# Sixty one-element vector writes ahead of the first transpose of a DMA-fed rotation kernel

## The chip, the cores and the metric

The kernel runs on one core of a Trainium2 chip. The metric is the device time of one execution in microseconds (us); lower is better. It reads about 1.8 us more than the span that the profile shows (124.01 us against 122.2 us for the profiled run of the kernel before). The vector engine is called DVE. The engines whose queues issue transfers are SP (here all loads but two) and ACT (here all stores, and two early loads).

## The reference

The program turns 96 images of 256 x 256 32-bit numbers by 90 degrees. It is pure data movement: 25.17 MB in and 25.17 MB out.

```python
def setup_inputs():
    batch, c, h, w = 32, 3, 256, 256
    return {"x": np.random.randn(batch, c, h, w).astype(np.float32)}

def reference(x):
    return np.rot90(x, k=1, axes=(-2, -1)).astype(np.float32)
```

## The kernel before

The 96 images are cut into six groups of 16 (4 MB each). A group is loaded into a tile `S`, transposed on the DVE in blocks into a tile `U`, and stored from `U`. The rest of the rotation lies in the address patterns. Three buffers exist for each of `S` and `U`. The first and the last group (kind 1) work in four 1 MB parts with one large transpose each. The four groups between (kind 2) use two 2 MB loads, 16 small transposes and two 2 MB stores. I call the transposes of kind 1 large and those of kind 2 small, and number the groups 0 to 5.

```python
    in_pool = ctx.enter_context(tc.tile_pool(name="in_pool", bufs=3))
    out_pool = ctx.enter_context(tc.tile_pool(name="out_pool", bufs=3))

    for g, kind in enumerate(KINDS):          # KINDS = [1, 2, 2, 2, 2, 1]
        S = in_pool.tile([P, F], fp32, name="S")
        U = out_pool.tile([P, F], fp32, name="U")
        if kind == 1:
            # ... (views cut)
            for s in range(4):
                eng = nc.scalar if g == 0 and s % 2 else nc.sync
                eng.dma_start(out=Sv[:, s], in_=xv[s])
            for s in range(4):
                # ... (src and dst: views of Sv[:, s] and Uv[:, s])
                nc.vector.transpose(dst, src)
                nc.scalar.dma_start(out=ov[s], in_=Uv[:, s])
        else:
            # ... (views cut)
            for b in range(2):
                nc.sync.dma_start(out=Sv[:, b], in_=xv[b])
            for q in range(R):                # R = 16
                nc.vector.transpose(dst[:, q], src[:, q])
            for a in range(2):
                nc.scalar.dma_start(out=ov[a], in_=Uv[:, a])
```

The framework schedules these instructions: it orders each engine's list by its own estimate of when things are ready, and it adds the semaphore waits.

## Time and profile before

| | before |
|---|---|
| time, median of the first 3 runs | 124.03 us (123.91 to 124.1) |
| span in the profile | 122.2 us |
| DVE busy | 91.5 us (75%) |
| bytes moved | 50.34 MB, mean 412 GB/s |

These are lines of the page of the kernel before. The DMA row gives, for each of 40 equal slices of the span, how busy the 16 DMA engines were in tenths (9 means 90% or more); the DVE row does so for the DVE.

```profile
span 122.2 us, 172 instructions
DVE 91.5 (75%) x72; POOL 0.2 (0%) x4
DVE  0039999729999999996599993199999999548000
DMA  4999999999999999999999999999999999999993
DMA packets 4610, 50.34 MB, mean 412 GB/s; under 512 B 513, under 2 KB 513, under 8 KB 513
```

The DMA row has no hole between its first and its last slice; the DVE row has five. The DVE's timeline puts times to them. Its columns are start, length from the first start to the last end, engine, line, operation, output and input, how many, and in brackets how long the engine sat idle before and what ended that.

```profile
8.17 15.44 DVE L50 STREAM_TRANSPOSE U<-S 128x2048 f32<-128x2048 f32 x4 [8.17 <-DMA S<-in_x_dram]
26.77 30.22 DVE L66 STREAM_TRANSPOSE U<-S 128x512 f32<-128x512 f32 x32 [3.16 <-DMA S<-in_x_dram]
59.34 15.20 DVE L66 STREAM_TRANSPOSE U<-S 128x512 f32<-128x512 f32 x16 [2.35 <-DMA S<-in_x_dram]
78.88 15.20 DVE L66 STREAM_TRANSPOSE U<-S 128x512 f32<-128x512 f32 x16 [4.33 <-issue]
93.93 11.61 DVE L50 STREAM_TRANSPOSE U<-S 128x2048 f32<-128x2048 f32 x3
108.69 3.97 DVE L50 STREAM_TRANSPOSE U<-S 128x2048 f32<-128x2048 f32 x1 [3.15 <-DMA S<-in_x_dram]
```

The DVE waits 8.17 us for the first load and then 3.16, 2.35, 4.33 and 3.15 us. The DMA engines hardly wait at all. The table of stretches shows it for the longest run of transposes; its columns are the stretch, its length, busy time of DVE and POOL (with the number of instructions), granted clock, DMA share and GB/s.

```profile
26.80:57.00 30.20, 30.19 (x32) 0.00 (x0) 1.00 1.01 432
```

### The profile page before, as it was taken

Reading aid. Unit: us, or ns where it says so; the run is one execution under the profiler, and the core shown is the slowest. Engines: PE = TensorE matmul, PEld = TensorE weight load, DVE = VectorE, ACT = ScalarE, POOL = GpSimd, SP = SyncE. Lnnn points to the kernel's source line nnn. Section 1 sums busy time; section 2 is a strip of 40 time slices with the busy share of each in tenths; the row PEclk is TensorE's granted clock in tenths of the full one; section 3 lists DMA queues with packets and bytes.
Section 4 is the critical chain, followed back from the end, with each engine's and each line's share of the span. In section 5 each row is a group of like instructions: output and inputs, shape, how many; then the busy total and the mean of one; then the engine's idle time right before and its main releaser. Section 6 shows DMA issues by size and latency. Waiting matters only on the chain.

```text
span 122.2 us, 172 instructions
## 1 busy us (share of the span) xinstructions
DVE 91.5 (75%) x72; POOL 0.2 (0%) x4
## 2 busy tenths in 40 slices
DVE  0039999729999999996599993199999999548000
POOL 0000000000000000000000000000000000000000
DMA  4999999999999999999999999999999999999993
GB/s 83 418 426 429 445 343 432 464 424 402 426 469 397 429 434 434 429 429 434 429 440 429 429 434 434 424 418 445 418 432 445 402 453 410 464 426 397 426 429 142
DMA packets 4610, 50.34 MB, mean 412 GB/s; under 512 B 513, under 2 KB 513, under 8 KB 513
## 3 DMA queue, kind: packets, MB, share of 16 engines
q10 hardware_dynamic: 2592, 27.26, 52.5%
q1 hardware_dynamic: 2016, 23.07, 45.2%
q14 instruction: 2, 0.01, 0.0%
HBM read 25.17 MB, written 25.17 MB: 412 GB/s over the span
## 4 chain that ended last, share of the span: by engine, by line
DMA 62%; DVE 27%; SPq 1%; issue 1%; DVEq 0%
DMA S<-in_x_dram 46%; DVE U L66 24%; DMA out_dram<-U 16%; DVE U L50 3%; SPq L45 1%; SPq L61 1%; DVEq L66 0%
## 5 line engine op out<-in xcount | busy, mean ns | idle before, releaser
L66 DVE STREAM_TRANSPOSE U<-S 128x512 f32<-128x512 f32 x64 | 60.6, 1050 | 9.8 <-DMA S<-in_x_dram 5.5
L50 DVE STREAM_TRANSPOSE U<-S 128x2048 f32<-128x2048 f32 x8 | 31.0, 3950 | 11.3 <-DMA S<-in_x_dram 11.3
L83 POOL MEMSET const-uint8-127<- 128x1 uint8 x1 | 0.1, 102 | 0.0
L83 POOL MEMSET const-bfloat16-1.0<- 128x1 bf16 x1 | 0.1, 101 | 0.0
L83 POOL MEMSET const-float32-0.0<- 128x1 f32 x1 | 0.1, 98 | 0.2 <-issue 0.2
L83 POOL MEMSET const-float32-1.0<- 128x1 f32 x1 | 0.1, 98 | 0.0
## 6 DMA issues: line engine op xcount, KB each, us to landing
S<-in_x_dram SPq DMA_DIRECT2D x8, 2048.0 KB, 25.0
out_dram<-U ACTq DMA_DIRECT2D x8, 2048.0 KB, 18.0
out_dram<-U ACTq DMA_DIRECT2D x8, 1024.0 KB, 15.0
S<-in_x_dram SPq DMA_DIRECT2D x6, 1024.0 KB, 26.5
S<-in_x_dram ACTq DMA_DIRECT2D x2, 1024.0 KB, 9.9
```

Source lines behind the costliest of these rows:

```text
L45: eng.dma_start(out=Sv[:, s], in_=xv[s])
L50: nc.vector.transpose(dst, src)
L61: nc.sync.dma_start(out=Sv[:, b], in_=xv[b])
L66: nc.vector.transpose(dst[:, q], src[:, q])
L83: nc = _bacc.Bacc("TRN2", target_bir_lowering=False, num_devices=1)
```

## The change

The intent is to put 60 tiny writes, with no use of their own, on the DVE ahead of its first transpose, and to see what they cost.

```diff
     out_pool = ctx.enter_context(tc.tile_pool(name="out_pool", bufs=3))
+
+    spare = ctx.enter_context(tc.tile_pool(name="spare", bufs=1)).tile([1, 1], fp32, name="spare")
+    for i in range(60):
+        nc.vector.memset(spare, 0.0)
```

All 60 write the same element, so each but the first waits on a semaphore for the one before. They do not all end up ahead of the first transpose: the scheduler places 31 ahead of it, one after each of the first three large transposes, and 26 between the fourth and the first small one.

## The prediction

> **What bounds the kernel.** DMA. The page moves 50.34 MB at a mean of 412 GB/s; its DMA row by slices stands at 9 tenths from slice 2 to 39, and a table of stretches gives 431-432 GB/s while the DVE transposes (26.8-57.0, 59.3-74.5, 78.9-109.0 us). 50.34 MB at 432 GB/s is 116.5 us of the 122.2 us span; the rest is start and tail. The DVE is busy 91.5 us (75%) and idle five times (timeline): 8.17 us before its first transpose, 3.16 at 26.77, 2.35 at 59.34, 4.33 at 78.88, 3.15 at 108.69. The chain of waits is 62% DMA, 27% DVE; the DVE part from 26.77 to 57.0 is on it only because the next load waits for a free buffer, while loads already queued keep the DMA full. The Trainium skill, "DMA: Bandwidth & Descriptors", section "Issuing engines are not separate DMA queues", says that all issuers share the same 16 DMA engines; the trace agrees (DMA share at most 1.02). So only the byte count and gaps in DMA work set the time.
>
> **What the change does.** It adds 60 one-element DVE memsets; bytes, transposes and DMAs stay. In the built order 31 stand ahead of the first transpose, one between each pair of the first four, and 26 between the fourth and the first small transpose. Nearly every memset waits on the DVE's own semaphore, so they run in series.
>
> **Cost.** No DVE memset is in the trace. POOL memsets last 98-102 ns; a transpose's end reaches the DMA issue in about 0.05 us (start 8.17, 3.95 long, issue at 12.17). The Trainium skill, "Perfetto Trace Analysis", section "Optimizing Scalar/DVE Operations", gives about 60 ns for a DVE access to SBUF, twice that in the profile. Estimate from these: 0.17 us per memset in series (0.06 to 0.25), 10 us for 60.
> - 31 ahead: from about 0.7 to 6 us, inside the 8.17 us wait: free.
> - 3 between: the fourth transpose ends about 0.4 us later, and so do stores.
> - 26 after: from about 24.0 to 28.4 us; the load they'd have waited for lands at 26.67. The first small transpose begins 1.6 us later (0 to 4).
>
> **How much is on the critical path.** That 1.6 us reaches the end of the second small group (57.0 to 58.6 us), then goes into the 2.35 us wait at 59.34; what passes goes into the 4.33 us at 78.88. Meanwhile the DMA stays fed: when the first group's stores are issued (42.0), the last earlier store lands at 45.8 and loads in flight at 49.5 and 59.2; when the later load and stores are issued (57.0), others land at 59.2 to 78.7. Nothing reaches the end.
>
> **Prediction: 124.1 us**, range 123.5 to 125.0; faster 0.01, same 0.97, slower 0.02.
>
> **What the profile would show.** DVE busy up by 3-8 us; 60 memsets of about 0.1 us, 0.1-0.25 us start to start; first transpose still at 8.2 us, its wait still ended by the load; first small transpose at about 28.4 us with its wait gone; the wait near 59 us under 1 us; DMA row and bytes as before; last load landing within 0.5 us of 108.7.
>
> **What would make it wrong.** Memsets over 0.24 us in series: the first transpose is late too, and the later shift exceeds 3.6 us. A delayed store or load that lets the DMA go dry, or another interleaving of the two queues that lands the last load later: the tail after it (13.5 us) follows one for one.

## The result, and the profile after

The changed kernel took 124.02 us (median of 6 runs, 123.94 to 124.19), the kernel before 123.97 us (6 runs, 123.91 to 124.1). The ratio is 1.0003, with a 95% interval of 0.999 to 1.0016. A ratio is the mean time of one kernel's fast runs over that of the other's of the same rounds, so not quite the ratio of the medians. The two kernels take the same time.

These are the page's lines of the changed kernel that answer to those above. The last one is the group of the writes: count, busy time, mean length in ns, idle time before them.

```profile
span 122.2 us, 231 instructions
DVE 95.1 (78%) x132; POOL 0.2 (0%) x4
DVE  3239999859999999997399996099999999766000
DMA  4999999999999999999999999999999999999993
DMA packets 4609, 50.34 MB, mean 412 GB/s; under 512 B 512, under 2 KB 512, under 8 KB 512
L37 DVE MEMSET spare<- 1x1 f32 x60 | 3.5, 59 | 3.8 <-PEq L89 0.8
```

The DVE is 3.6 us busier, and the DMA row is the same digit for digit. The DVE's timeline of the changed kernel up to the second group of waits:

```profile
0.79 3.46 DVE L37 MEMSET spare<- 1x1 f32 x31 [0.79 <-PEq L89]
8.14 7.84 DVE L56 STREAM_TRANSPOSE U<-S 128x2048 f32<-128x2048 f32 x2 [3.89 <-DMA S<-in_x_dram]
...
19.79 6.78 DVE L37 MEMSET spare<- 1x1 f32 x27
26.92 30.40 DVE L72 STREAM_TRANSPOSE U<-S 128x512 f32<-128x512 f32 x32 [0.35 <-DMA S<-in_x_dram]
60.08 15.21 DVE L72 STREAM_TRANSPOSE U<-S 128x512 f32<-128x512 f32 x16 [2.76 <-DMA S<-in_x_dram]
```

The first 31 writes end at 4.25 us (0.79 + 3.46), inside the wait for the first load, which shrinks from 8.17 to 3.89 us of idle time. The next transpose starts at 8.14 us as before. The 27 of the other line (the one after the third transpose, and the 26) end at 26.57 us, and the first small transpose starts at 26.92 us against 26.77 us. One write in the chain takes (3.46 - 0.06) / 30 = 0.113 us from start to start, though it is only 0.059 us long.

So the writes as built delay the first small transpose by only about 0.2 us. (The third small group starts 0.7 us later, at 60.08 us; the second traces below come back to it.) That leaves two explanations of why it is free:

- **Theory (spare time, DMA bound).** The DMA engines set the time. The DVE may be late by microseconds as long as they do not run dry; its later waits take the delay up.
- **Rival (a close fit).** The writes are free only because they end 0.1 us before the DVE may go on anyway. Any more would come out one for one.

### The profile page after: what moved, and what is told of

Its sections match the earlier page's. It is cut to its first block, busy times and chain, and to the rows that moved or that the text cites. A ratio compares the mean times of both kernels' runs of the same rounds, so it can differ in the third digit from the quotient of the medians.

```text
span 122.2 us, 231 instructions
## 1 busy us (share of the span) xinstructions
DVE 95.1 (78%) x132; POOL 0.2 (0%) x4
## 4 chain that ended last, share of the span: by engine, by line
DMA 67%; DVE 15%; issue 10%; SPq 0%
DMA S<-in_x_dram 51%; DMA out_dram<-U 15%; DVE U L72 8%; DVE U L56 7%; SPq L51 0%; DVE spare L37 0%
## 5 line engine op out<-in xcount | busy, mean ns | idle before, releaser
L37 DVE MEMSET spare<- 1x1 f32 x60 | 3.5, 59 | 3.8 <-PEq L89 0.8
```

Source lines behind the costliest of these rows:

```text
L37: nc.vector.memset(spare, 0.0)
```

## The experiments

Nine kernels were built on the kernel before. All results were correct.

### 44 and 60 writes between the first two groups

```diff
+            if g == 1:
+                for i in range(60):            # e_mid60; 44 in e_mid44
+                    nc.vector.memset(dst[0:1, :, 0, 0, 0], 0.0)
             for q in range(R):
                 nc.vector.transpose(dst[:, q], src[:, q])
```

Each write touches one element in every piece that the 16 transposes write, so none of these can start before all writes are done.

> All 60 writes (16 elements each, in one chain) stand between the fourth large transpose and the first small one. Theory (spare time of the DVE in later waits): 60 x 0.113 = 6.8 us from about 23.6 to 30.4, the first small transpose begins near 30.4 instead of 26.8 (3.6 us late), the 2.4 us wait near 59 vanishes, the 4.3 us wait near 79 shrinks by about 1 us, the DMA row stays full, time 124.0 (+-0.3). Rival (one for one: the writes were free only because they ended 0.1 us before the load they share the gap with landed): 127.6 us.

Measured (run e_mid60): 123.89 us against 124.0 us, ratio 0.9992 (0.9977 to 1.0006). The first small transpose started at 31.68 us, 4.9 us late (a 16-element write took 0.140 us from start to start, not 0.113). The rival's one for one is wrong. But the scheduler, seeing the writes, had also assigned the completion semaphores of several transfers anew, so loads waited for other things than before. The second run takes that away: with 44 writes, order and waits of all transfers are those of the kernel before.

> As e_mid60 with 44 writes: the count up to which the order and the waits of every DMA stay those of the kernel before, so that only the delay differs. In e_mid60 one write took 139 ns start to start, so 44 end at 23.4 + 6.1 = 29.5 us and the first small transpose is 2.7 us late. Theory: the 2.2 us wait near 59 takes it up, the one near 79 the rest, DMA row full, time 124.0 (+-0.3). Rival (e_mid60 was free only because its DMA waits were arranged anew; with the old ones the delay comes out one for one): 126.7 us.

Measured (e_mid44): 124.1 us against 123.96 us, ratio 1.0009 (0.9992 to 1.0025). Here is the DVE's timeline of this run:

```profile
8.56 15.44 DVE L50 STREAM_TRANSPOSE U<-S 128x2048 f32<-128x2048 f32 x4 [8.56 <-DMA S<-in_x_dram]
23.93 6.11 DVE L67 MEMSET U<- 1x16 f32 x44
30.08 45.26 DVE L69 STREAM_TRANSPOSE U<-S 128x512 f32<-128x512 f32 x48
76.65 15.17 DVE L69 STREAM_TRANSPOSE U<-S 128x512 f32<-128x512 f32 x16 [1.31 <-issue]
91.70 11.58 DVE L50 STREAM_TRANSPOSE U<-S 128x2048 f32<-128x2048 f32 x3
105.73 3.97 DVE L50 STREAM_TRANSPOSE U<-S 128x2048 f32<-128x2048 f32 x1 [2.44 <-DMA S<-in_x_dram]
```

The first small transpose is 3.3 us late (30.08 against 26.77), and not 2.7 as expected; in this trace the first transpose itself starts 0.4 us later than in that of the kernel before (8.56 against 8.17), after the wait for its load. Then 48 small transposes run in one piece where the kernel before had 32, a wait, and 16: the wait near 59 us is gone. The wait near 79 us has shrunk from 4.33 to 1.31 us. The fourth small group and the last transpose even start *earlier* than before: 76.65 against 78.88 us, and 105.73 against 108.69 us (107.54 in a second trace of the kernel before). The DVE's delay holds back stores, and loads that are already queued land earlier; a likely reason is that they then get more of the shared DMA engines, but no run tells that apart from other effects. The page's DMA row of this run:

```profile
DMA  4999999999999999999999999999999999999993
```

It is the row of the kernel before. The theory holds, in the clean case. What this run does not show is a delay too long for the later waits of the DVE to take up: those of the kernel before add up to 9.8 us after the first small transpose.

### 60 and 120 writes forced ahead of the first transpose

```diff
+            if g == 0:
+                for i in range(120):           # 60 in e_ahead60
+                    nc.vector.memset(Uv[0:1, :, 0:1], 0.0)
             for s in range(4):
                 # src, dst
                 nc.vector.transpose(dst, src)
```

> All 60 writes really ahead of the first transpose (4 elements each, one chain): they end at 0.8 + 60 x 0.113 = 7.6 us, before the load lands at 8.1. Theory and rival agree on 124.0; the first transpose at 8.2, the first small one at 26.8, so no trace of the writes after 8 us.

Measured (e_ahead60): 123.89 us against 124.01 us, ratio 0.9986 (0.9971 to 1.0001). The writes ended at 7.93 us and the first transpose started at 8.48 us, after a wait that the load ended. That is later than the expected 8.2, but in the traces with no write ahead of it the first transpose starts anywhere from 7.79 us (e_wait120) to 8.56 us (e_mid44). So 60 writes fit into the first wait; this run does not part the theories.

> 120 writes (4 elements each, one chain), all ahead of the first transpose: first transpose at 0.8 + 120 x 0.113 = 14.4 us instead of 8.2, so all stores of the first group 6.2 us late. Theory: the 16 DMA engines have 12.6 MB of loads (29 us) queued without any store, so they don't run dry; the 6.2 us go into the waits at 26.8, 59 and 79 (3.2 + 2.4 + 4.3 us); time 124.0 to 124.5. Rival (one for one beyond the first wait): 130.2 us.

Measured (e_ahead120): 124.56 us against 124.0 us, ratio 1.0047 (1.0032 to 1.0062). The first transpose started at 15.17 us, 7.0 us late (a 4-element write took 0.120 us from start to start), and 0.56 us of that reached the end. The rival's 130.2 us is far off. The theory's upper end, 124.5 us, was just missed. The 64 small transposes now run without any wait (from the timeline of this run):

```profile
0.79 14.34 DVE L48 MEMSET U<- 1x4 f32 x120 [0.79 <-PEq L86]
15.17 15.44 DVE L53 STREAM_TRANSPOSE U<-S 128x2048 f32<-128x2048 f32 x4
30.50 60.29 DVE L69 STREAM_TRANSPOSE U<-S 128x512 f32<-128x512 f32 x64
```

In both of these runs the scheduler had also rearranged the waits of transfers, so where the 0.56 us came from stays open.

### 60 writes without the chain

```diff
+    spare = ctx.enter_context(tc.tile_pool(name="spare", bufs=1)).tile([1, 60], fp32, name="spare")
+    for i in range(60):
+        nc.vector.memset(spare[:, i:i + 1], 0.0)
```

> 60 one-element writes to 60 different elements, so none waits on the one before; all stand ahead of the first transpose. If the 113 ns start to start of the changed kernel came from the chain of semaphore waits: about 60 ns start to start or less, the last write near 4.5 us. If it is the engine's own cost: still 113 ns, the last near 7.5 us. Time 124.0 either way, the first transpose at 8.2 us with its wait ended by the load.

Measured (e_free60): 123.97 us against 124.01 us, ratio 1.001 (0.9978 to 1.0042). From the timeline of this run:

```profile
0.79 1.72 DVE L34 MEMSET spare<- 1x1 f32 x60 [0.79 <-PEq L86]
8.69 15.44 DVE L53 STREAM_TRANSPOSE U<-S 128x2048 f32<-128x2048 f32 x4 [6.17 <-DMA S<-in_x_dram]
```

All 60 end at 2.51 us: (1.72 - 0.06) / 59 = 0.028 us each from start to start, though a record is still 0.059 us long, so they overlap. The chain costs the difference, 0.113 - 0.028 = 0.085 us per write. The expectation was about 0.06 us from start to start, or less. The first transpose started at 8.69 us and not at 8.2, 6 us after the last write and still after a wait that the load ended.

### The same writes after the last load

If DVE time is free because the DMA engines are busy meanwhile, it must cost something where they are about to run out of work: after the last load. A one-element copy that reads the last load makes the writes wait for it. Order and waits of all transfers are those of the kernel before.

```diff
+                if g == 5 and s == 3:
+                    nc.vector.tensor_copy(Uv[0:1, 3, 0:1], Sv[0:1, 3, 0:1])
+                    for i in range(60):        # 30 in e_tail30, 120 in e_tail120
+                        nc.vector.memset(Uv[0:1, 3, 0:1], 0.0)
                 nc.vector.transpose(dst, src)
```

> The same 60 one-element writes, but after the last load has landed (a one-element copy reads it first) and before the last transpose. Theory: last transpose 6.9 us late (115.6 instead of 108.7), its store issued at 119.6 instead of 112.7, when the other stores have just landed, so alone: about 4.5 us to landing, end of the span near 124.8 instead of 122.2, time near 126.5 (+2.0%, range 125.8 to 128). Rival A (DVE writes are free anywhere because DMA bounds the kernel): 124.0. Rival B (one for one): 130.9.

Measured (e_tail60): 125.62 us against 124.0 us, ratio 1.0127 (1.0112 to 1.0142): less than 2%, but clear of the noise. Rival A (free anywhere) and rival B (one for one) are both wrong. It is 0.2 us below the theory's range: the lone last store took 3.8 us from issue to landing, not 4.5, and was issued at 119.18 us, not 119.6. The last store of the kernel before was issued at 112.7 us and took 8.7 us, with other stores still under way. That gives landings at 121.4 and 123.0 us, 1.6 us apart, and the medians are 1.6 us apart. The table of stretches of this run shows the DMA engines run dry (share in the column before the last):

```profile
116.00:117.00 1.00, 1.00 (x1) 0.00 (x0) 1.00 1.06 451
117.00:118.00 1.00, 1.00 (x1) 0.00 (x0) 1.00 0.68 287
118.00:119.00 1.00, 1.00 (x1) 0.00 (x0) 1.00 0.04 16
119.00:120.00 1.00, 0.15 (x1) 0.00 (x0) 1.00 0.00 0
120.00:121.00 1.00, 0.00 (x0) 0.00 (x0) 1.00 1.07 451
```

The same stretches of the kernel before have no such hole:

```profile
118.00:119.00 1.00, 0.00 (x0) 0.00 (x0) 1.00 0.99 418
119.00:120.00 1.00, 0.00 (x0) 0.00 (x0) 1.00 0.98 418
```

> As e_tail60 with 120 writes. Theory: the spare time of the tail is used up by the first 60, so the second 60 come out one for one: 6.8 us over e_tail60, near 133.3 us. Rival A: 124.0. Rival B: 137.7.

Measured (e_tail120): 132.39 us against 124.0 us, ratio 1.0693 (1.0662 to 1.0723). That is 0.9 us under the expected time, as e_tail60 had been. The second 60 writes cost 132.39 - 125.62 = 6.77 us, and 60 x 0.113 is 6.78. Once the DMA engines are dry, a write costs its full time.

> As e_tail60 with 30 writes. Theory (a threshold: the last store costs nothing as long as it is issued before the DMA engines run dry near 117.7 us): store issued at 112.7 + 3.4 = 116.1, time 124.0 (+-0.4). Rival (a cost per write, 1.6 us / 60 = 0.027 us each): 124.8 us.

Measured (e_tail30): 123.98 us against 123.96 us, ratio 1.0001 (0.9986 to 1.0015). Lines of this run's DVE timeline and table of stretches:

```profile
108.20 3.34 DVE L53 MEMSET U<- 1x1 f32 x30
111.57 3.97 DVE L54 STREAM_TRANSPOSE U<-S 128x2048 f32<-128x2048 f32 x1
118.00:119.00 1.00, 0.00 (x0) 0.00 (x0) 1.00 0.97 410
119.00:120.00 1.00, 0.00 (x0) 0.00 (x0) 1.00 1.04 442
```

The DMA engines stay busy where they ran dry in e_tail60. So it is a threshold and not a price per write: 30 writes after the last load (3.34 us of DVE time) cost nothing, 60 cost 1.6 us, 120 cost 8.4 us. An estimate from these: if each write past the threshold costs its full 0.113 us, the 1.6 us are 14 writes, so the threshold lies near 46 writes, with the last store issued near 117.6 us. That is where the DMA share of e_tail60 begins to fall.

This run also parts two things that the theory had put together. Between these writes and the end no wait of the DVE is left that could take their 3.34 us up, and still they were free. So what makes them free is the DMA work that is still queued; a later wait of the DVE is not needed for it.

> As e_tail120, but the one-element copy ahead of the 120 writes reads the third transpose's result and not the last load, so the writes start at about 105.6 and the 3.2 us wait for the last load lies under them. Theory: 3.1 us less than e_tail120, near 130.2 us (last transpose near 119.3). Rival (only the number of writes in the tail counts, not the wait they stand in): the same as e_tail120.

The edit is that of e_tail120, but the copy reads `Uv[0:1, 2, 0:1]`. Measured (e_wait120): 129.59 us against 124.01 us, ratio 1.0443 (1.0414 to 1.0473). That is 2.8 us less than e_tail120 for the same instructions, moved into the wait just ahead (0.3 us less than expected). In the trace the last transpose starts at 118.87 us instead of 121.85.

### Second traces

> The kernel before, unchanged, for a second trace: how far the waits near 59, 79 and 108.7 us move from one execution to the next with nothing changed. If by 0.7 us or more, then the changed kernel's 60.08 (59.34 before) and 108.03 (108.69 before) are no effect of the writes. Time 124.0.

One look (e_same) at 124.06 us, its state unknown as there was only one run. The last transpose started at 107.54 us (108.69 in the first trace), but the third small group again near 59.35:

```profile
59.35 15.20 DVE L66 STREAM_TRANSPOSE U<-S 128x512 f32<-128x512 f32 x16 [2.21 <-DMA S<-in_x_dram]
```

> The changed kernel again, for a second trace: whether the third small group begins at 60.1 us again (then the shift from 59.35, which two traces of the kernel before agree on, goes with the change) or near 59.35 (then it was one execution's).

One look (e_after2) at 124.05 us, state unknown too:

```profile
60.13 15.20 DVE L72 STREAM_TRANSPOSE U<-S 128x512 f32<-128x512 f32 x16 [2.76 <-DMA S<-in_x_dram]
```

So the third small group of the changed kernel starts some 0.8 us later in both of its traces than in both of the kernel before. The start of the last transpose (108.03 and 107.52 us against 108.69 and 107.54) moves by up to 1.15 us between executions of the same kernel. The first shift goes with the change in these four traces. It is small, though: in the other runs that leave everything before 60 us as it was (those with writes in the tail) this group starts anywhere from 58.90 us (e_wait120) to 59.58 us (e_tail30). How the small shift of the stores leads to it (the fourth store is issued at 23.75 instead of 23.64 us) was not tried. Neither reaches the end.

## Why the prediction was right or wrong

- **The time: right.** 124.1 us was predicted and 124.02 measured. Alone this says little for the argument: the delay of 1.6 us that it was meant to take up never came, because the 26 writes happened to end just before the load landed. That was luck; the argument itself was tested by e_mid44 and the runs in the tail, and held.
- **What bounds the kernel: right.** The time does not follow the DVE. A DVE that is 3.3 us late at unchanged transfers leaves it at 124.1 us (e_mid44), while the DMA row does not change. A hole in the DMA work in the tail costs 1.6 us (e_tail60). The Trainium skill says in "DMA: Bandwidth & Descriptors", section "Issuing engines are not separate DMA queues", that transfers of all issuers interleave on the same 16 engines. The trace of the kernel before agrees: with SP and ACT transfers queued the share is 1.01 and the rate 432 GB/s (26.8 to 57.0 us).
- **31 writes ahead are free: right.** The wait for the first load ended as before, at 8.14 us. They ended at 4.25 us and not near 6.
- **The cost of a write: mis-sized.** The prediction said "0.17 us per memset in series (0.06 to 0.25), 10 us for 60". It was 0.113 us, inside the range, so 6.8 us for 60; a record was 0.059 us long, where about 0.1 had been expected. The Trainium skill's "Perfetto Trace Analysis", section "Optimizing Scalar/DVE Operations", gives about 60 ns of busy time per access and about twice that in the profile. For a one-element write both came out at about half: 28 ns from start to start without the chain, and a record of 59 ns.
- **The 26 after the fourth transpose: wrong in size.** The prediction had the first small transpose at "28.4 us with its wait gone". It came at 26.92 us, as 26 x 0.113 = 2.9 us fits into the 3.16 us wait. So the delay of 1.6 us did not happen (its range, 0 to 4 us, holds the 0.15 measured), and "the wait near 59 us under 1 us" read 2.76 us. This step was also not needed: in e_mid44 a delay of 3.3 us did happen and was taken up in the two places that the prediction named.
- **The three between: mis-sized.** The fourth large transpose's store was issued 0.11 us later and not 0.4, since a write overlaps the transposes around it.
- **"Last load landing within 0.5 us of 108.7": wrong, narrowly.** The last transpose, which waits for it, started at 108.03 us. The kernel before shifts by 1.15 us between two traces, so this was a bad sign to name.
- **"The tail after it (13.5 us) follows one for one": wrong.** The prediction said this of a last load that lands later. In e_tail30 the writes put 3.3 us between the last load and the last transpose, and the time stayed at 123.98 us: the tail has spare time as long as stores are queued. It did not matter for the changed kernel, whose last load landed no later.
- **DVE busy up by 3 to 8 us: right** (3.6), and no change of the DMA row or the bytes: right.

## What to carry to other kernels

Before costing an added instruction, ask whether the resource that sets the time, here the DMA engines, has queued work while it runs; if so, expect it to be free, or nearly, up to the point where that queue runs dry (here a delay of 3.3 us in the middle cost nothing, and one of 7.0 us at the start 0.56 us, which stays unexplained). Find that point by experiment at the place where it is nearest, here the tail: 30 writes after the last load cost nothing, and from 60 to 120 every further write cost its full 0.113 us. Here a write that waits for the one before cost four times one that does not (0.113 against 0.028 us), so let scratch writes go to different elements.

## What the Trainium skill lacked or had wrong

- "VectorE: DVE Perf Modes", section "The DRAIN you can't avoid", reports eight copies with a semaphore after each as fast as eight with one after the last only (13.88 us, so 1.7 us a copy), and says the semaphore costs nothing extra there. That does not carry over to one-element writes, for which the page gives no measurement with and without the wait: 0.113 us from start to start where each waits for the one before (31 in 3.46 us), 0.028 us where none does (60 in 1.72 us).
- "Perfetto Trace Analysis", section "Optimizing Scalar/DVE Operations", gives about 60 ns for a DVE access to SBUF as busy time and about twice that as the profiled length. A one-element write, which reads nothing, is recorded at 59 ns, and unchained ones start every 28 ns: the ratio of two is there, at half the size. The one-element copy of e_tail60, which also reads, is recorded at 142 ns, near twice the page's 60. The page does not tell the two apart.
- "DMA: Bandwidth & Descriptors", section "Where 436 GB/s comes from", says that transfers between HBM and SBUF are bound by the HBM side, about 358 GB/s per core. With loads and stores mixed, this one core moved 432 GB/s over 30 us, near the 435 GB/s that the same section gives for the fabric. Just above that section the same page calls 358 GB/s the share of a core while both cores of the pair stream, so it is the sentence that is too broad. Whether the other core of the pair was idle is not shown.
- I found no page on how much a delay of a compute engine costs in a kernel bound by DMA. Here it was none for 3.3 us in the middle and none for 3.3 us in the tail, but the full cost in the tail once the DMA share had fallen to 0 (0.113 us per write from 60 to 120 writes).
